# A two-layer trunk on one core: how the low parts of the weight tiles are made

## Chip, core and metric

The kernel runs on one core of a Trainium2 chip. The metric is the device time of one execution in microseconds. A time is the median of a few runs; a profile is one execution taken by the hardware profiler.

## What is computed

The reference is a trunk of two layers over 1024 tokens of width 1024, all in float32. The first layer mixes by a gated linear recurrence and by stick-breaking attention in parallel, the second by a gated convolution of 31 taps. After each mixer stands an MLP with squared ReLU, which holds most of the multiplications:

```python
def sq_relu_mlp(h, w1, w2):
    a = jax.nn.relu(h @ w1)
    return (a * a) @ w2

# D_MODEL = 1024, SEQ = 1024, D_FF = 4096, DEPTH = 2
for layer in range(DEPTH):
    if layer % 2 == 0:
        x = x + lru_sb_mixer(rms_norm(x, ev_norm_g[j]), ev_w_in[j], ..., ev_w_out[j])
    else:
        x = x + conformer_conv_module(rms_norm(x, od_norm_g[j]), od_pw1_w[j], ..., od_pw2_b[j])
    x = x + sq_relu_mlp(rms_norm(x, mlp_norm_g[layer]), mlp_w1[layer], mlp_w2[layer])
return rms_norm(x, final_g)
```

## The kernel before

The tokens are worked in two chunks, a and b, of 512. A float32 product is made of three passes of TensorE in the type float32r: every operand is split into a high part (its value in float32r) and a low part (what is left), and low x high, high x low and high x high are added in PSUM (`mm3`, lines 154 to 156).

A weight unit is 128 x 1024 elements. Two units are loaded at once by SP into a raw tile of 128 x 2048 (`raw`, two buffers). For each unit ScalarE casts the raw tile into the high part `wh` (line 101 for rows, 122 for columns), and VectorE subtracts the high part from the raw tile into the low part `wl` (lines 102 and 123). `wh` and `wl` have four buffers each. `col_units` loads column tiles (w1 of the MLP; pw, the first pointwise product of the convolution module; xg and qk, the first layer's input projection). For w1 the two column tiles lie next to each other in DRAM, so a partition of the raw tile holds, for each of 8 k tiles, 256 columns, of which a unit takes 128; for the others the two units are apart in the raw tile. `row_units` loads four row tiles of 512 columns (w2 of the MLP, wo, and q, the second pointwise product). The four units of v, at the start, are rows too.

The MLP (`mlp`) is run once for each layer and chunk: a0, b0, a1, b1, in the trace by chunk as w1a, w2a, w1b, w2b. A step m1 makes one of 32 hidden tiles from one unit of w1: 24 matmuls, then on ScalarE a relu, a square into float32r and a square in float32 (lines 249 to 252), then VectorE's low part of the activation (line 253). A step m2 adds four hidden tiles' product with half of the rows of w2, from two units: 48 matmuls and four adds into the residual on VectorE (line 237). After the first hidden tiles the steps run in groups: m2, m2, m1, m1, m1, m1.

The 30 later taps of each convolution tile (line 644) are put into a list, `waiting`, and `paced` issues some behind each of certain VectorE instructions: the number given to it is the credit of one such instruction.

The program is written in one order, and a scheduler puts the instructions of each engine into the order in which that engine runs them; an engine runs its own list strictly in order. A tile's buffer is given to the next tile of its kind when its last reader is done. GpSimd (POOL) has short work: the root of the norms (lines 184 to 186) and, in attention, a column of ones ahead of each scan (line 507) or a carried value (line 509).

Of the kernel before, what the change touches and what calls it, by code (L numbers as in the profile page):

```python
# [8 lines left out]
F32 = mybir.dt.float32  # L9
F32R = mybir.dt.float32r  # L10
BF16 = mybir.dt.bfloat16
AF = mybir.ActivationFunctionType
ALU = mybir.AluOpType
PSUM = bass.MemoryType.PSUM

P = 128
D = 1024
S = 1024
C = 512          # tokens in a chunk
NCH = S // C  # L20
KT = D // P      # k tiles of the model width
NH = 2           # halves of the model width
TT = C // P      # token tiles in a chunk
FF = 4096
KCONV = 31
HALO = KCONV - 1
G = 4            # hidden tiles in a group of the MLP
RMS_EPS = 1e-6
# [3 lines left out]
def tile_hybrid_trunk(  # L32
# [37 lines left out]

# [1 line left out]
    ident = cp.tile([P, P], F32, name="ident")  # L72
# [10 lines left out]

# [1 line left out]
    waiting, credit = [], [0.0]  # L85
# [7 lines left out]

# [1 line left out]
    def raw_tile(name):  # L95
        return wp.tile([P, 2048], F32, tag="raw", bufs=2, name=name)

    def split_w(raw, name):
        hi = wp.tile([P, 1024], F32R, tag="wh", bufs=4, name=f"wh_{name}")
        lo = wp.tile([P, 1024], F32R, tag="wl", bufs=4, name=f"wl_{name}")  # L100
        A.copy(hi, raw)  # L101
        paced(V.tensor_tensor(lo, raw, hi.bitcast(F32), op=ALU.subtract), 1)  # L102
        return hi, lo

    def col_units(w, c0, c1, name):
        """units of [k, 128 cols] for the col tiles from c0 and c1"""
        raw = raw_tile(f"raw_{name}")
        wk = w.rearrange("(k p) m -> p k m", p=P)
        if c1 == c0 + P:
            r3 = raw.rearrange("p (k m) -> p k m", k=KT)  # L110
            nc.sync.dma_start(r3, wk[:, :, c0:c0 + 2 * P])
            srcs = [r3[:, :, i * P:(i + 1) * P] for i in range(2)]
        else:
            r4 = raw.rearrange("p (i k m) -> p i k m", i=2, k=KT)
            srcs = [r4[:, i] for i in range(2)]
            for r, c in zip(srcs, (c0, c1)):
                nc.sync.dma_start(r, wk[:, :, c:c + P])

        def unit(i):
            hi = wp.tile([P, KT, P], F32R, tag="wh", bufs=4, name=f"wh_{name}{i}")  # L120
            lo = wp.tile([P, KT, P], F32R, tag="wl", bufs=4, name=f"wl_{name}{i}")
            A.copy(hi, srcs[i])  # L122
            paced(V.tensor_tensor(lo, srcs[i], hi.bitcast(F32), op=ALU.subtract), 2)  # L123
            return hi, lo
        return unit

    def row_load(w, k0, c0, name):
        """four k tiles, from row tile k0 or the ones listed"""
        raw = raw_tile(f"raw_{name}")
        ks = [k0 + i for i in range(4)] if isinstance(k0, int) else list(k0)  # L130
        i = 0
        while i < 4:
            n = 1
            while i + n < 4 and ks[i + n] == ks[i] + n:
                n += 1
            nc.sync.dma_start(raw[:, i * C:(i + n) * C].rearrange("p (k m) -> p k m", k=n),
                              w[ks[i] * P:(ks[i] + n) * P, c0:c0 + C].rearrange("(k p) m -> p k m", p=P))
            i += n
        return raw
# [5 lines left out]
    def row_units(w, k0, c0, name):  # L145
        """units of [2 k, 512 cols] for four k tiles from row tile k0"""
        raw = row_load(w, k0, c0, name)
        return row_unit(raw, 0, name) + row_unit(raw, 1, name)

    def mm3(acc, prs):  # L150
        """acc = sum over (lhsT hi/lo, rhs hi/lo) pairs, three passes each"""
        n = len(prs)
        for i, ((lh, ll), (rh, rl)) in enumerate(prs):
            T.matmul(acc, ll, rh, start=(i == 0), stop=False)  # L154
            T.matmul(acc, lh, rl, start=False, stop=False)  # L155
            T.matmul(acc, lh, rh, start=False, stop=(i == n - 1))  # L156
# [10 lines left out]

# [1 line left out]
    def rstd_of(xt, junk, name, vector=False):  # L169
        """xt: the two half tiles of 128 tokens; junk: scratch"""  # L170
        rs = sp.tile([P, 1], F32, tag="rs", name=f"rs_{name}")
# [17 lines left out]
    def norm(xt, g, g0, temp, name):  # L189
        """xt[token tile][half] -> the normed chunk, feature-major, split: [k] -> (hi, lo)"""  # L190
        res = []
        for _ in norm_parts(xt, g, g0, temp, name, TT, res):
            pass
        return res

    def norm_parts(xt, g, g0, temp, name, nt, res):
        """nt token tiles at a time, in steps of a feature tile"""
        rs = []
# [31 lines left out]

# [1 line left out]
    def rows_into_x(acts, ws, h, xt, name):  # L232
        for t in range(TT):
            acc = mm_ps(f"o_{name}{t}")
            mm3(acc, [((a[0][:, t * P:(t + 1) * P], a[1][:, t * P:(t + 1) * P]), w)
                      for a, w in zip(acts, ws)])
            paced(V.tensor_tensor(xt[t][h], acc, xt[t][h], op=ALU.add), 1.5)  # L237

# [1 line left out]
    def mlp(layer, hT, xt, name):  # L240
        acts, units = {}, {}

        def m1(f):
# [8 lines left out]
            A.activation(r, r, AF.Square)  # L252
            paced(V.tensor_tensor(lo, r, hi.bitcast(F32), op=ALU.subtract), 2.5)
            acts[f] = (hi, lo)
# [13 lines left out]

    NG = FF // (G * P)

    # ================= layer 0: recurrence and attention =================
    w_in = ev_w_in[0]
    y = [[None] * KT for _ in range(NCH)]      # [chunk][k tile], feature-major, split
    dp = ctx.enter_context(tc.tile_pool(name="dp", bufs=1, space=bass.MemoryType.DRAM))
    with tc.tile_pool(name="p1", bufs=1) as p1, tc.tile_pool(name="ps1", bufs=1, space=PSUM) as ps1:
# [16 lines left out]
        def load_vecs(groups, dma, name):  # L292
            """rows of 128 channels into columns"""
            rows = [(nm, ap.rearrange("a (k p) -> (a k) p", p=P)) for nm, ap in groups]
# [59 lines left out]

        # 4 * log_sigmoid(lam): min(lam, 0) - log1p(exp(-|lam|)), the log by its atanh series
        lam = vecs["lam"][0][:, vecs["lam"][1]:vecs["lam"][1] + 4]
# [23 lines left out]

        last = [None] * 4     # the previous chunk's last state

# [3 lines left out]
        def keep(c, k, t):  # L386
            """a k tile of the mixer's output: to DRAM, but for the last ones"""
            y[c][k] = t
# [4 lines left out]
        def lru(m, xr, gt):  # L393
# [3 lines left out]
            def decay(c):  # L397
# [8 lines left out]
                A.activation(nt[c], pr, AF.Sigmoid, bias=vec("ga_b", m))  # L406
                # t = tanh(log_a / 2): a = (1 + t) / (1 - t), 1 - a^2 = -4 t / (1 - t)^2
                A.activation(nt[c], nt[c], AF.Tanh, scale=c4[:, m:m + 1])
# [33 lines left out]
            with tc.high_priority(offset=140):  # L442
                decay(0)
                gate(0)
                ins = decay(1)
            # the square roots of both chunks together, for one load of their table
            with tc.issue_after(ins.ins):
# [29 lines left out]
        def attention(c, hp, q1, q2, ks):  # L477
            av = ps1.tile([P, C], F32, tag="av", bufs=1, name=f"av{hp}{c}")
            order = None
            for tt in range(TT):  # L480
# [3 lines left out]
                while hi_s > 0:  # L484
# [5 lines left out]
                    for j in range(2):  # L490
# [4 lines left out]
                        with tc.high_priority(offset=1000):  # L495
                            T.matmul(z[:, :w], q1[j][:, ts_], k_[:, :w], start=True, stop=False)
                            T.matmul(z[:, :w], q2[hs, ts_], k_[hs, :w], start=False, stop=not diag)  # L497
                            if diag:
                                T.matmul(z[:, w - P:w], ident_b, mask, start=False, stop=True)
                        # the product of keep over the later keys, then times beta: the weights  # L500
                        ke = at(f"ke{nm}")
# [19 lines left out]
                        wts.append(ke)  # L521
                    # one token tile's sums at a time in the bank
                    with tc.issue_after(order) if order is not None else nullcontext():
# [12 lines left out]
        def qk_cols(hp):  # L536
            """split for products of two passes: q1 holds the high part twice, q2 the low part,
            ks the high and the low part"""
            u = col_units(w_in, 1024 + hp * P, 1536 + hp * P, f"qk{hp}")
# [28 lines left out]

# [1 line left out]
        def out_proj(cs, i, h):  # L570
# [35 lines left out]

    # ================= layer 1 pieces =================
    halo = cp.tile([P, KT, HALO], F32, name="halo")
# [26 lines left out]
    def conv(c, ms, u, cv):  # L635
        """put the taps of some channel tiles, in turn, among the waiting"""
        for m in ms:
# [10 lines left out]
    def layer_norm(c, cv, s):  # L648
        """steps; s gets the split result"""
        xh = []  # L650
# [60 lines left out]

    # ================= schedule of the two chunks =================
    def steps(todo, n=None, between=()):
        """run the list's steps up to the group n's second hidden tile, with others in between"""
        between = list(between)
# [74 lines left out]
```

## Time and profile before

| | |
|---|---|
| median of 3 runs | 2253.16 us (2252.9 to 2256.04) |
| profiled execution, span | 2252.2 us |
| TensorE, matmuls | 2219.5 us, 99% |
| VectorE | 1414.6 us, 63% |
| ScalarE | 953.6 us, 42% |
| GpSimd | 98.3 us, 4% |
| all DMA | 199.24 MB |

The page gives the profiled execution's span and no other time of it; the median of the runs is 1.0 us above the span. Busy times are sums over an engine's instructions. A matmul's end is modelled, and successive matmuls overlap: one of 512 columns is shown with 0.39 us and the next starts 0.23 us later. So the distance of two starts is what a matmul costs. In the timeline a row has its start, its duration, the engine, the line, the operation and the tiles, and in brackets the idle time before it with what ended it.

### The profile page before, as it was taken

What the parts mean: (1) busy time and instruction counts of PE and PEld (TensorE: products, weight loads), DVE (VectorE), ACT (ScalarE), POOL (GpSimd) and SP (SyncE); (2) the same over time, 40 slices, a digit from 0 to 9 for tenths busy, and PEclk for the clock granted to TensorE, in tenths of its full rate; (3) what the DMA queues carried; (4) which work ended last, traced back from release to release, by engine and by line L of the source; (5) the groups of instructions that cost most, each with busy time, mean ns of one, the idle gap of its engine ahead of it and who ended that gap; (6) DMA issues with size and microseconds to landing.
All of it is one profiled execution on the core that took longest, in us unless ns stands there. A gap on an engine that the chain in (4) does not pass through costs nothing.

```text
span 2252.2 us, 25937 instructions
## 1 busy us (share of the span) xinstructions
PE 2219.5 (99%) x10180; PEld 1768.3 (79%) x10180; DVE 1414.6 (63%) x1934; ACT 953.6 (42%) x1506; POOL 98.3 (4%) x280
## 2 busy tenths in 40 slices
PE   7999999999999999999999999999999999999998
PEld 5866766678888888888888888788888888888886
DVE  4376777866443444579889765899886555444344
ACT  4456566555333333433333363433333545333332
POOL 1000000001000000200000010300000001000000
PEclk9999999999999999999999999999999999999999
DMA  4211002312222232432222223322222224222222
GB/s 157 56 41 36 34 29 85 117 38 75 94 94 93 94 104 92 114 94 94 94 94 94 94 94 94 84 94 94 94 94 94 94 94 146 97 94 94 94 94 75
DMA packets 172009, 199.24 MB, mean 88 GB/s; under 512 B 5648, under 2 KB 120688, under 8 KB 171888
## 3 DMA queue, kind: packets, MB, share of 16 engines
q1 hardware_dynamic: 171872, 197.59, 27.4%
q8 instruction: 80, 1.31, 0.2%
q14 instruction: 41, 0.34, 0.0%
q10 hardware_dynamic: 16, 0.00, 0.0%
HBM read 190.23 MB, written 7.34 MB: 88 GB/s over the span
## 4 chain that ended last, share of the span: by engine, by line
PE 95%; DVE 2%; ACT 1%; issue 1%; DMA 0%; POOL 0%; SPq 0%; DVEq 0%; POOLq 0%; ACTq 0%
PE o_a L154 5%; PE o_a L156 5%; PE o_b L155 5%; PE o_b L154 5%; PE o_b L156 5%; PE o_a L155 5%; PE m_a L154 5%; PE m_b L155 5%; PE m_a L156 5%; PE m_a L155 5%; PE m_b L156 5%; PE m_b L154 5%; PE av L527 2%; PE z L497 1%; PE o_wo L154 1%; PE wt L519 1%
## 5 line engine op out<-in xcount | busy, mean ns | idle before, releaser
L644 DVE SCALAR_TENSOR_TENSOR cv<-u,dwT,cv 128x512 f32<-128x512 f32 x480 | 340.6, 757 | 0.2
L154 PE MATMUL o_a<-wh_w2a,al_a 128*128 128x512 f32 x512 | 202.8, 396 | 0.0
L155 PE MATMUL o_a<-wl_w2a,ah_a 128*128 128x512 f32 x512 | 202.7, 396 | 0.0
L156 PE MATMUL o_b<-wh_w2b,ah_b 128*128 128x512 f32 x512 | 202.6, 396 | 0.0
L154 PE MATMUL o_b<-wh_w2b,al_b 128*128 128x512 f32 x512 | 202.6, 396 | 0.0
L155 PE MATMUL o_b<-wl_w2b,ah_b 128*128 128x512 f32 x512 | 202.5, 396 | 0.0
L156 PE MATMUL o_a<-wh_w2a,ah_a 128*128 128x512 f32 x512 | 202.1, 396 | 0.0
L122 ACT CAST wh_w1b<-raw_w1b 128x1024 fp32r<-128x1024 f32 x64 | 67.3, 1052 | 220.5 <-PE o_b L156 210.6
L122 ACT CAST wh_w1a<-raw_w1a 128x1024 fp32r<-128x1024 f32 x64 | 67.3, 1053 | 214.1 <-PE o_a L156 204.0
L102 DVE TENSOR_TENSOR wl_w2a<-raw_w2a,wh_w2a 128x1024 fp32r<-128x1024 f32 x64 | 78.3, 1224 | 122.9 <-ACT wh_w2a L101 122.8
L102 DVE TENSOR_TENSOR wl_w2b<-raw_w2b,wh_w2b 128x1024 fp32r<-128x1024 f32 x64 | 81.1, 1268 | 117.2 <-ACT wh_w2b L101 117.1
L237 DVE TENSOR_TENSOR xr<-o_a,xr 128x512 f32<-128x512 f32 x128 | 87.7, 688 | 81.5 <-PE o_a L156 81.4
L237 DVE TENSOR_TENSOR xr<-o_b,xr 128x512 f32<-128x512 f32 x128 | 88.0, 688 | 77.2 <-PE o_b L156 77.1
L156 PEld LDWEIGHTS o_b<-wh_w2b,ah_b 128*128 128x128 f32 x512 | 96.2, 188 | 23.1
L156 PEld LDWEIGHTS o_a<-wh_w2a,ah_a 128*128 128x128 f32 x512 | 96.3, 188 | 23.0
L155 PEld LDWEIGHTS o_b<-wl_w2b,ah_b 128*128 128x128 f32 x512 | 96.2, 188 | 22.9
L154 PEld LDWEIGHTS o_a<-wh_w2a,al_a 128*128 128x128 f32 x512 | 96.2, 188 | 22.9
L154 PEld LDWEIGHTS o_b<-wh_w2b,al_b 128*128 128x128 f32 x512 | 96.2, 188 | 22.8
L155 PEld LDWEIGHTS o_a<-wl_w2a,ah_a 128*128 128x128 f32 x512 | 96.3, 188 | 22.7
L249 ACT ACTIVATE r_b<-m_b 128x512 f32<-128x512 f32 x64 | 38.3, 599 | 167.2 <-PE m_b L156 167.2
L249 ACT ACTIVATE r_a<-m_a 128x512 f32<-128x512 f32 x64 | 38.3, 599 | 162.8 <-PE m_a L156 162.8
L123 DVE TENSOR_TENSOR wl_w1b<-raw_w1b,wh_w1b 128x1024 fp32r<-128x1024 f32 x64 | 78.0, 1221 | 38.2 <-ACT wh_w1b L122 38.2
(535 smaller groups left out, 5327.4 us busy)
## 6 DMA issues: line engine op xcount, KB each, us to landing
raw_w1a<-in_mlp_w_dram SPq DMA_DIRECT2D x32, 1024.0 KB, 5.3
raw_w2a<-in_mlp_w_dram SPq DMA_DIRECT2D x32, 1024.0 KB, 5.0
raw_w1b<-in_mlp_w_dram SPq DMA_DIRECT2D x32, 1024.0 KB, 5.4
raw_w2b<-in_mlp_w_dram SPq DMA_DIRECT2D x32, 1024.0 KB, 5.0
raw_pw<-in_od_pw_w_dram SPq DMA_DIRECT2D x32, 512.0 KB, 5.4
raw_q<-in_od_pw_w_dram SPq DMA_DIRECT2D x8, 1024.0 KB, 5.0
raw_wo<-in_ev_w_out_dram SPq DMA_DIRECT2D x6, 768.0 KB, 5.4
xa<-in_x_dram SPq DMA_DIRECT2D x16, 256.0 KB, 5.4
```

What stands on the lines that cost most here:

```text
L102: paced(V.tensor_tensor(lo, raw, hi.bitcast(F32), op=ALU.subtract), 1)
L122: A.copy(hi, srcs[i])
L123: paced(V.tensor_tensor(lo, srcs[i], hi.bitcast(F32), op=ALU.subtract), 2)
L154: T.matmul(acc, ll, rh, start=(i == 0), stop=False)
L155: T.matmul(acc, lh, rl, start=False, stop=False)
L156: T.matmul(acc, lh, rh, start=False, stop=(i == n - 1))
L237: paced(V.tensor_tensor(xt[t][h], acc, xt[t][h], op=ALU.add), 1.5)
L249: A.activation(r, acc, AF.Relu)
L497: T.matmul(z[:, :w], q2[hs, ts_], k_[hs, :w], start=False, stop=not diag)
L519: T.transpose(pt[:, b * P:(b + 1) * P], ke[:, b * P:(b + 1) * P], ident)
L527: ins = T.matmul(av[j * 64:j * 64 + 64, tt * P:(tt + 1) * P], vt[lo_s // P + b][:, hc:hc + 64], wts[j][:, b * P:(b + 1) * P], start=(diag ...
L644: waiting.append(lambda k=k, m=m: V.scalar_tensor_tensor(cv[m], u[m][:, k:k + C], dwT[:, k * KT + m:k * KT + m + 1], cv[m], op0=ALU.mult, ...
```

## The change

For all weight units but those of v, VectorE's subtraction goes. A new function, `rest`, takes its place: ScalarE copies the high part with scale -1 into the low part's tile, and a DMA issued by GpSimd adds the raw tile to it. 332 units are made so. As the subtractions no longer stand on VectorE, they no longer give credit to the taps, and the credits of the residual's add and of the activation's low part are raised. Nothing else of the computation is changed.

```diff
+    def rest(lo, raw, hi):
+
+        A.activation(lo, hi.bitcast(F32), AF.Copy, scale=-1.0)
+        Q.dma_start(lo, raw, accum_op=ALU.add)
+
     def split_w(raw, name):
...
         A.copy(hi, raw)
-        paced(V.tensor_tensor(lo, raw, hi.bitcast(F32), op=ALU.subtract), 1)
+        if name[0] == "v":
+            V.tensor_tensor(lo, raw, hi.bitcast(F32), op=ALU.subtract)
+        else:
+            rest(lo, raw, hi)
         return hi, lo
...
             A.copy(hi, srcs[i])
-            paced(V.tensor_tensor(lo, srcs[i], hi.bitcast(F32), op=ALU.subtract), 2)
+            rest(lo, srcs[i], hi)
             return hi, lo
...
-            paced(V.tensor_tensor(xt[t][h], acc, xt[t][h], op=ALU.add), 1.5)
+            paced(V.tensor_tensor(xt[t][h], acc, xt[t][h], op=ALU.add), 2.5)
...
-            paced(V.tensor_tensor(lo, r, hi.bitcast(F32), op=ALU.subtract), 2.5)
+            paced(V.tensor_tensor(lo, r, hi.bitcast(F32), op=ALU.subtract), 6)
```

The scheduler's order moves with it. ScalarE in a group of the last MLP, from the second m1 step to the casts of the two units for the second m2 step (r_b, ah_b: relu and squares of a hidden tile; the numbers are the program's own and differ from one program to the other). Before:

```order
L249 ACTIVATE r_b_15969<-m_b_15940 128x512
L101 CAST wh_w2b_16056<-raw_w2b_16050 128x1024
L251 ACTIVATE ah_b_15971<-r_b_15969 128x512
L252 ACTIVATE r_b_15969<-r_b_15969 128x512
L249 ACTIVATE r_b_16005<-m_b_15976 128x512
L251 ACTIVATE ah_b_16007<-r_b_16005 128x512
L252 ACTIVATE r_b_16005<-r_b_16005 128x512
L101 CAST wh_w2b_16118<-raw_w2b_16116 128x1024
L249 ACTIVATE r_b_16043<-m_b_16014 128x512
L101 CAST wh_w2b_16122<-raw_w2b_16116 128x1024
```

ScalarE at the same place in the changed program (line 106 is the cast, line 100 the negation, 257 to 260 are the relu and the squares), first around the cast of the second unit of the first m2 step:

```order
L106 CAST wh_w2b_15213<-raw_w2b_15211 128x1024
L257 ACTIVATE r_b_15128<-m_b_15098 128x512
L106 CAST wh_w2b_15218<-raw_w2b_15211 128x1024
L100 ACTIVATE wl_w2b_15214<-wh_w2b_15213 128x1024
L259 ACTIVATE ah_b_15130<-r_b_15128 128x512
L100 ACTIVATE wl_w2b_15219<-wh_w2b_15218 128x1024
L260 ACTIVATE r_b_15128<-r_b_15128 128x512
```

and then around the two units of the second m2 step:

```order
L257 ACTIVATE r_b_15204<-m_b_15174 128x512
L259 ACTIVATE ah_b_15206<-r_b_15204 128x512
L106 CAST wh_w2b_15281<-raw_w2b_15279 128x1024
L106 CAST wh_w2b_15286<-raw_w2b_15279 128x1024
L260 ACTIVATE r_b_15204<-r_b_15204 128x512
L100 ACTIVATE wl_w2b_15282<-wh_w2b_15281 128x1024
L100 ACTIVATE wl_w2b_15287<-wh_w2b_15286 128x1024
```

The negation of a unit does not follow its cast at once: the other unit's cast stands between them, and for the first m2 step a relu too.

GpSimd in attention, in the third head pair (ke: the tile that gets its column of ones; xgt and lh: other short copies). Before:

```order
L507 MEMSET ke_2601 128x1
L507 MEMSET ke_2616 128x1
L507 MEMSET ke_2630 128x1
L507 MEMSET ke_2648 128x1
L507 MEMSET ke_2663 128x1
L470 COPY xgt_3093<-xgt_3065 128x3
L507 MEMSET ke_2684 128x1
L438 COPY lh_2416<-xc_2374 128x1
```

and in the changed program (line 101 is the DMA, 515 the column of ones):

```order
L515 MEMSET ke_2613 128x1
L101 DMA wl_qk_3309<-raw_qk_3232 128x1024
L515 MEMSET ke_2628 128x1
L515 MEMSET ke_2642 128x1
L515 MEMSET ke_2660 128x1
L515 MEMSET ke_2675 128x1
L478 COPY xgt_3106<-xgt_3078 128x3
L515 MEMSET ke_2696 128x1
L101 DMA wl_wo_3905<-raw_wo_3901 128x1024
L446 COPY lh_2426<-xc_2384 128x1
```

The issues of the accumulating DMAs stand among the columns of ones. ScalarE loads a function table 12 times in the changed program and 10 times before.

## Rows read from the trace of the kernel before

**Rows 1.** The page: busy time of the engines, and the chain's shares.
```profile
PE 2219.5 (99%) x10180; PEld 1768.3 (79%) x10180; DVE 1414.6 (63%) x1934; ACT 953.6 (42%) x1506; POOL 98.3 (4%) x280
...
PE 95%; DVE 2%; ACT 1%; issue 1%; DMA 0%; POOL 0%; SPq 0%; DVEq 0%; POOLq 0%; ACTq 0%
```

**Rows 2.** Waits of TensorE: in total, times, longest.
```profile
PE nps_e L211 <- DVE xn_e L206: 8.3, 2, 7.1
...
PE nps_ma L211 <- DVE hl_ma L217: 2.9, 2, 2.6
```

**Rows 3.** Stretches: length, busy time of each engine, clock, DMA share, GB/s.
```profile
120.00:520.00 400.00, 394.97 (x2069) 276.85 (x2070) 296.54 (x434) 236.07 (x466) 20.05 (x114) 1.00 0.17 56
1440.00:1460.00 20.00, 17.10 (x81) 13.52 (x80) 20.00 (x20) 8.24 (x11) 11.24 (x7) 1.00 0.29 79
1890.00:2235.00 345.00, 345.00 (x1502) 281.66 (x1501) 139.60 (x160) 121.94 (x164) 3.51 (x6) 1.00 0.29 95
```

**Rows 4.** Groups by line: VectorE's subtraction; count, busy, mean ns, idle before.
```profile
L102 DVE TENSOR_TENSOR wl_w2a<-raw_w2a,wh_w2a 128x1024 fp32r<-128x1024 f32 x64 | 78.3, 1224 | 122.9 <-ACT wh_w2a L101 122.8
```

**Rows 5.** Timeline of ScalarE in the last MLP.
```profile
1939.45 1.05 ACT L122 CAST wh_w1b<-raw_w1b 128x1024 fp32r<-128x1024 f32 x1 [8.74 <-PE o_b L156]
...
1946.85 1.05 ACT L101 CAST wh_w2b<-raw_w2b 128x1024 fp32r<-128x1024 f32 x1
...
1951.76 0.60 ACT L249 ACTIVATE r_b<-m_b 128x512 f32<-128x512 f32 x1 [2.67 <-PE m_b L156]
1952.25 1.04 ACT L101 CAST wh_w2b<-raw_w2b 128x1024 fp32r<-128x1024 f32 x1
1953.19 0.63 ACT L251 ACTIVATE ah_b<-r_b 128x512 fp32r<-128x512 f32 x1
...
1959.60 1.05 ACT L101 CAST wh_w2b<-raw_w2b 128x1024 fp32r<-128x1024 f32 x1 [0.48 <-DMA raw_w2b<-in_mlp_w_dram]
1962.64 0.60 ACT L249 ACTIVATE r_b<-m_b 128x512 f32<-128x512 f32 x1 [1.99 <-PE m_b L156]
...
1983.64 1.05 ACT L122 CAST wh_w1b<-raw_w1b 128x1024 fp32r<-128x1024 f32 x1 [8.74 <-PE o_b L156]
```

**Rows 6.** Timeline of SP, VectorE and TensorE in the same group.
```profile
1941.79 13.16 SPq L136 DMA_DIRECT2D raw_w2b<-in_mlp_w_dram  x2
...
1953.33 1.23 DVE L102 TENSOR_TENSOR wl_w2b<-raw_w2b,wh_w2b 128x1024 fp32r<-128x1024 f32 x1 [3.51 <-ACT wh_w2b L101]
...
1960.68 1.23 DVE L102 TENSOR_TENSOR wl_w2b<-raw_w2b,wh_w2b 128x1024 fp32r<-128x1024 f32 x1 [0.83 <-ACT wh_w2b L101]
...
1973.88 0.39 PE L155 MATMUL o_b<-wl_w2b,ah_b 128*128 128x512 f32 x1
...
1975.28 0.39 PE L155 MATMUL o_b<-wl_w2b,ah_b 128*128 128x512 f32 x1
```

**Rows 7.** The page: DMA queue; issues by tile with KB and us to landing.
```profile
q1 hardware_dynamic: 171872, 197.59, 27.4%
...
raw_w1a<-in_mlp_w_dram SPq DMA_DIRECT2D x32, 1024.0 KB, 5.3
raw_w2a<-in_mlp_w_dram SPq DMA_DIRECT2D x32, 1024.0 KB, 5.0
...
out_dram<-fo SPq DMA_DIRECT2D x16, 256.0 KB, 2.0
```

**Rows 8.** Groups by line on GpSimd: longest instruction, and a short one.
```profile
L694 POOL TENSOR_TENSOR xr<-xr,pw2b 128x512 f32<-128x512 f32 x16 | 25.8, 1646 | 23.1 <-DVE hl_ma L217 15.9 <-DMA pw2b<-in_od_pw_b_dram 7.3
...
L186 POOL TENSOR_TENSOR rs_f<-rs_f,mhalf 128x1 f32<-128x1 f32 x8 | 4.4, 550 | 0.7
```

**Rows 9.** Groups by line on ScalarE: loading a function table.
```profile
L503 ACT ACT_TABLE_LOAD x4 | 5.1, 1283 | 0.2 <-PE av L527 0.2
```

**Rows 10.** The chain in order of time, in attention: start, us, what.
```profile
382.00 0.95 ACT wh_wo L101
...
389.69 0.31 ACT ke L503
```

## Prediction

> **What bounds the kernel now.** I read the page's busy table first, then the waits of TensorE, then stretches, then one group of the MLP in time order. TensorE is busy 99% of the span, and the chain that ended last is 95% TensorE [rows 1]. Its own named waits are a few microseconds each; the longest is on the norm at the start, and after 520 us only the one on nps_ma is over 1 us [rows 2]. Over the last MLP, 1890 to 2235 us, it is busy 345.00 of 345.00 us while VectorE, from which the change takes work, is busy 139.60 [rows 3]. So shorter VectorE work has little to give. What can change the time is whether a low part still arrives before TensorE asks for it.
>
> **What is removed and added.** VectorE loses 332 subtractions (64 each for the four w1 and w2 groups, 32 for pw, 16 for q, 12 for wo, 8 each for xg and qk; the 4 of v stay) at about 1.22 us [rows 4], some 405 us of its 1414.6. ScalarE gains 332 negations of 128x1024. The nearest row is the cast of the same shape, 1.05 us [rows 5]: 349 us, which takes it from 953.6 to about 1300 of 2252 us. GpSimd's queue gains 332 accumulating DMAs of 512 KB, the only new kind of work. 332 times 512 KB is 174 MB against 197.59 MB now, which took 27.4% of the sixteen engines [rows 7]; counted as twice the bytes, since both operands are read, it is another 48%. The engines are not full. Latency is the question, not the total.
>
> **The path of a low part.** Before: cast, subtraction. After: cast, negation, GpSimd's issue, DMA. I call d the time from the end of a negation to the landing of its sum. No row shows it. From below: the rate in the queue's row is 197.59 MB in 27.4% of 16 x 2252.2 us, 20 GB/s an engine, 320 GB/s in all; a 256 KB store lands in 2.0 us [rows 7], of which 0.82 is data at that rate, so 1.18 us is fixed, and 512 KB would be 1.18 + 1.64 = 2.8 us. From above: two operands read are 1 MB, and a 1 MB load lands in 5.0 us [rows 7]; with GpSimd's longest instruction, 1.65 us, ahead of it that is 6.65 us [rows 8]. For w1 the raw piece of a partition is cut into 8 runs of 512 B (the raw tile holds two column tiles side by side). Eight of GpSimd's short instructions, 0.55 us each [rows 8], would be 4.4 us, and d there 9.4 us at most. I take 5.0 + 0.5 = 5.5 us for both kinds, nearest to the row that moves as many bytes, behind one short GpSimd instruction.
>
> The Trainium skill, DMA: Bandwidth & Descriptors, section Anatomy of one DMA — SWDGE (gpsimd) path, fits a GpSimd-issued DMA with about 2.0 us plus bytes over 436 GB/s. By that fit, as an estimate, d would be 3.2 us and the sum would be that of the first rival below; no run here shows such a DMA. Collectives: The Full Stack (the Trainium skill), section The bandwidth ceiling: the fold count and why AG ≠ RS ≠ AR, says that a DMA that adds runs at about half the rate of one that copies, because of two source reads. With that, an estimate, d is 4.4 us, still the rival.
>
> **How much d is hidden.** I follow one group of the last MLP. A group is four m1 steps and two m2 steps: its third m1 unit is cast at 1939.45 and the next group's at 1983.64, 44.2 us apart [rows 5]. Two m1 steps lie between the relus at 1951.76 and 1962.64 [rows 5], 5.44 us each, which leaves 11.2 us for an m2 step. A0, A1 and B0, B1 are the two units of its two m2 steps. Both raw tiles of w2 and the second w1 pair go in turn through one raw buffer: B's load starts only when A1's low part is there. Before, A1 is subtracted at 1953.33 for 1.23 us [rows 6], B's load follows, B0's cast is at 1959.60 [rows 5] and its subtraction ends at 1961.91 [rows 6]. TensorE first reads that low part at 1973.88 and B1's at 1975.28 [rows 6]: 12 us to spare.
>
> After, with ScalarE in its new order (ScalarE's fences in the section on the change): A1's cast still waits for the relu at 1951.76 and runs at 1952.25 [rows 5], ending 1953.29. Then stand A0's negation (1.05), a square (0.63 [rows 5]) and A1's negation (1.05), to 1956.02. So A0's negation, whose cast was done long before, is queued behind a cast that waits for TensorE. The DMA lands at 1956.02 + d. The load of B takes 5.06, from 1941.79 [rows 6] to the cast at 1946.85 [rows 5] in the load before it. Then two casts (2.10), a square (0.63) and B0's negation (1.05): 1964.86 + d, and landed 1964.86 + 2d; B1 at 1965.91 + 2d. Against 1973.88 and 1975.28 the slack is 9.0 - 2d and 9.4 - 2d. **The point from which it decides is d = 4.5 us**; each microsecond above costs two in a group. One more loop: A's load waits for the low part of the third m1 unit, cast at 1939.45 [rows 5], negated by 1941.55, landed 1941.55 + d. With load and cast A0 is ready at 1947.66 + d, and this pushes A1 from d = 4.6 on, one for one.
>
> At d = 5.5 a group stalls TensorE by 2 x 5.5 - 9.0 + 5.5 - 4.6 = 2.9 us. The four MLPs have 8 groups each, 32: **+92 us**. At the lower bound it is 0; at the upper ones 2 x 6.65 - 9.0 + 9.4 - 4.6 = 9.1 us a group, +291. Each stall moves the rest of the program, because TensorE has no idle to take it up. Elsewhere I cost it at nothing: in pw each unit is wanted three units of 5.44 us after its buffer is free, and in q and wo the steps of 11.2 us have no load waiting for a sum just ahead of them; both cover 2.1 + 5.5 us. If that cover is gone (d above 9), they stall too.
>
> **Attention.** ScalarE is busy 236.07 of the 400 us from 120 to 520 [rows 3]; 28 negations (xg, qk, wo) and, by the new order, two more table loads (12 instead of 10) of 1.28 us [rows 9] come to 32 us there. At most all of it lies on the path, at least nothing. The chain is ScalarE's alone from a wh_wo cast at 382.00 to 389.69 [rows 10]; three negations and the two loads there make 3 x 1.05 + 2 x 1.28 = 5.7, so I take **+6 us**. GpSimd's column of ones for a scan now stands behind DMA issues (its fences); those issues wait for a negation, and VectorE's scan for the column. That is in the 0 to 32.
>
> **What is won.** From 1440 to 1460 us VectorE is busy 20.00 of 20.00 and TensorE only 17.10 [rows 3]: subtractions of pw stand between the taps. They leave, and I take **-3 us**; the most would be that and TensorE's other VectorE waits after 60 us, some 8 in all. The pacing gives 44 taps a group instead of 34 (6 x 4 + 2.5 x 8 against 4.5 x 4 + 8 x 2); 44 taps of 0.7 us with the adds still fit into 44 us, so no gain or loss is put down.
>
> **Sum:** 2252.2 + 92 + 6 - 3 = 2347.2 us of span; the median of the runs, 2253.16, is 1.0 above the span, so **2348 us**.
>
> **Rival 1, the sums land in time (not slower).** d is below 4.5. For it: the store's row gives 2.8 us. Against it: stores read one operand only, and no GpSimd issue is in them. Then the MLPs lose nothing, attention gives 0 to 15, pw up to -8: 2245 to 2268 us, about 2256 in the middle. It ends faster only if attention is hidden too; then the 20 us at 1440 decide, at about 2248.
>
> **Rival 2, GpSimd or the pieces are the bound.** d for w1 is near 9.4 and for rows near 6.65. For it: eight times the pieces in 128 DMAs. Against: loads of w1 with 1 KB runs land as fast as those of w2 with longer ones, 5.3 and 5.0 us [rows 7]. Price: +291 + 6 - 3, 2547 us; more if GpSimd needs over 11 us for each of the four w1 units of a group, since it then fills the 44 us itself.
>
> **Rival 3, the change does not unload VectorE** as it says, because taps and adds set its order anyway. TensorE does not wait for it, so this gives the time of rival 1.
>
> **How the numbers follow.** About 0.2%, 4.5 us, is what a measurement of this kernel can tell from no change. The forecast (d 4.5 to 6.5, 2268 to 2490 us) has a chance of 0.43; rival 1 with rival 3, 0.34; rival 2, 0.23, half of it above 2550. Of the 0.34, 0.09 is faster than 2248.7, 0.17 within 0.2%, 0.08 slower. So faster 0.09, same 0.17, slower 0.74. The range leaves out half of rival 2 and most of the faster cases: 2250 to 2550.
>
> **What would show it.** Right: TensorE gets waits on wl_w2 low parts, each of 2 to 4 us and once a group, at the second m2 step of it; B's raw load is issued some 9 us after A1's cast begins instead of 2.3; VectorE falls to about 1010 us and ScalarE rises to about 1300. Wrong: no wait of TensorE on a low part (then d is under 4.5 and rival 1 holds); waits before m1 steps or GpSimd busy for most of the MLP (rival 2); a loss that sits before 520 us (then the attention term is the one that is mis-sized).

## The result, and the profile after

The changed kernel takes **2600.28 us** (median of 4 runs, 2597.99 to 2602.44); the kernel before, beside it, 2253.03 us. The ratio is 1.154, 95% interval 1.152 to 1.155: 347 us slower. The forecast was 2348 us in a range up to 2550, so the direction held and the size did not.

The page of the kernel after: busy time of the engines, the DMA queues, and the shares of the chain that ended last (compare [rows 1] and [rows 7]).

```profile
PE 2345.5 (90%) x10180; PEld 1822.2 (70%) x10180; DVE 1025.7 (40%) x1602; ACT 1268.0 (49%) x1840; POOL 466.5 (18%) x612
...
q0 software_dynamic: 162496, 174.08, 46.5%
q1 hardware_dynamic: 171872, 197.59, 23.5%
...
DMA 44%; PE 35%; issue 12%; POOL 4%; ACT 4%; DVE 1%; POOLq 0%; SPq 0%; DVEq 0%; ACTq 0%
```

VectorE fell to 1025.7 and ScalarE rose to 1268.0 us, close to the 1010 and 1300 foretold: the change does unload VectorE. But the chain, 95% TensorE before, is now 44% DMA. The new queue q0 has the share that was estimated, 46.5% against 48%. Over the span as a whole no engine and no queue is full, and still 344 us were added.

Waits of TensorE in the kernel after: in total, times, longest (compare [rows 2]).

```profile
PE o_a L163 <- DMA wl_w2a<-raw_w2a: 60.0, 35, 3.5
PE o_b L163 <- DMA wl_w2b<-raw_w2b: 57.9, 39, 4.3
PE m_b L162 <- DMA wl_w1b<-raw_w1b: 41.4, 14, 6.4
PE m_a L162 <- DMA wl_w1a<-raw_w1a: 29.0, 12, 5.1
```

The waits on low parts of w2 are there, of up to 4.3 us, as foretold (and in the group followed below B's load leaves 9.75 us after A1's cast begins, where some 9 were foretold); beside them stand waits of up to 6.4 us on low parts of w1, which the forecast did not have. They add up to 188 us. Another 126 us are TensorE's busy time itself, 2345.5 for 2219.5 [rows 1], on the same 10180 matmuls; the granted clock in the next view goes with it.

Stretches of the kernel after: length, busy time of PE, PEld, DVE, ACT and POOL, granted clock, DMA share, GB/s (compare [rows 3]; 2250 to 2307 is one group of the last MLP, 2258 to 2276 the part of it with three sums of w1).

```profile
120.00:520.00 400.00, 391.42 (x2022) 273.68 (x2021) 269.75 (x406) 254.51 (x485) 33.73 (x127) 0.98 0.29 76
...
2250.00:2307.00 57.00, 48.35 (x189) 37.79 (x189) 8.11 (x12) 22.67 (x28) 9.67 (x8) 0.91 0.78 149
...
2258.00:2276.00 18.00, 14.21 (x52) 11.19 (x51) 1.38 (x2) 7.64 (x9) 4.64 (x3) 0.81 1.01 148
```

In this group the granted clock is no longer 1.00 but 0.91, a mean of pieces at 2.4 and at 1.2 GHz: behind a wait of 3.79 us that ends at 2267.54, matmuls start 0.43 us apart until 2272.8 us, and 0.23 us apart after that. So some of the waits cost more than their own length on TensorE. Whether that also lengthens the span depends on who sets the group, and that is the next question.

**Who sets the group.** SP's own waits, in total, times, longest: two rows of the kernel before, then the same loads after.

```profile
SPq L136 <- DVE wl_w1a L123: 190.9, 18, 12.3
...
SPq L136 <- DVE wl_w2b L102: 124.6, 16, 11.9
```

```profile
SPq L144 <- DMA wl_w2b<-raw_w2b: 268.8, 16, 19.0
...
SPq L144 <- DMA wl_w1a<-raw_w1a: 252.2, 18, 19.3
```

Loads always waited for a raw buffer. What frees it was VectorE's subtraction and is now the landing of an accumulating DMA. The chain in order of time shows what follows (kernel after, one group of the last MLP; start us, us, what; TensorE's pieces left out).

```profile
2250.39 7.32 DMA raw_w1b<-in_mlp_w_dram
...
2262.26 9.53 DMA wl_w1b<-raw_w1b
2271.92 7.15 DMA raw_w2b<-in_mlp_w_dram
...
2284.29 5.87 DMA wl_w2b<-raw_w2b
...
2300.12 6.74 DMA wl_w2b<-raw_w2b
2307.00 7.39 DMA raw_w1b<-in_mlp_w_dram
```

SP's issues of the two row loads in the same group (start us, us, operation; A leaves at 2271.92, B at 2290.28), to be read against the 13.16 us of [rows 6].

```profile
2271.92 18.73 SPq L144 DMA_DIRECT2D raw_w2b<-in_mlp_w_dram  x2
```

It is a closed loop. One of the two raw buffers takes, in turn, one pair of w1 tiles, row half A and row half B, while the other buffer holds the other pair, whose last unit is split only after both row halves. From one w1 load to the next are 2307.00 - 2250.39 = 56.61 us, and they consist of three times the same: a load (7.40, 7.17, 5.12 us until the cast starts), ScalarE's two casts and two negations with GpSimd's pick-up (4.47, 5.20, 4.72), and the second sum until the next load leaves (9.66, 5.99, 6.88). Loads 19.7, ScalarE 14.4, sums 22.5: together 56.6. TensorE needs 44.2 for the group, so it is not the bound there any more. (From 2290.29 to 2300.10 the page's chain runs through TensorE's matmuls. I read the sum that leaves at 2300.12 as released by its negation, which ends at 2299.83: the other two sums, too, leave 0.29 and 0.30 us behind theirs.) A slower clock or a longer TensorE step should then not show in the span as long as it fits into the loop; that was not tried by itself.

### The profile page after: what moved, and what is told of

Its sections match the earlier page's. It is cut to its first block, busy times and chain, and to the rows that moved or that the text cites. A ratio compares the mean times of both kernels' runs of the same rounds, so it can differ in the third digit from the quotient of the medians.

```text
span 2596.3 us, 27011 instructions
## 1 busy us (share of the span) xinstructions
PE 2345.5 (90%) x10180; PEld 1822.2 (70%) x10180; DVE 1025.7 (40%) x1602; ACT 1268.0 (49%) x1840; POOL 466.5 (18%) x612
## 3 DMA queue, kind: packets, MB, share of 16 engines
q0 software_dynamic: 162496, 174.08, 46.5%
## 4 chain that ended last, share of the span: by engine, by line
DMA 44%; PE 35%; issue 12%; POOL 4%; ACT 4%; DVE 1%; POOLq 0%; SPq 0%; DVEq 0%; ACTq 0%
DMA wl_w2b<-raw_w2b 6%; DMA raw_w2a<-in_mlp_w_dram 6%; DMA raw_w2b<-in_mlp_w_dram 6%; DMA wl_w2a<-raw_w2a 6%; DMA wl_w1b<-raw_w1b 5%; DMA wl_w1a<-raw_w1a 5%; DMA raw_w1b<-in_mlp_w_dram 4%; DMA raw_w1a<-in_mlp_w_dram 3%; PE av L535 2%; PE wt L527 1%; PE z L505 1%; PE xg L162 1%; PE xg L163 1%; PE xg L164 1%; PE o_wo L162 1%
## 5 line engine op out<-in xcount | busy, mean ns | idle before, releaser
L163 PE MATMUL o_a<-wl_w2a,ah_a 128*128 128x512 f32 x512 | 215.8, 422 | 60.0 <-DMA wl_w2a<-raw_w2a 60.0
L106 ACT CAST wh_w2b<-raw_w2b 128x1024 fp32r<-128x1024 f32 x64 | 65.7, 1044 | 277.9 <-DMA raw_w2b<-in_mlp_w_dram 277.9
L261 DVE TENSOR_TENSOR al_b<-r_b,ah_b 128x512 fp32r<-128x512 f32 x64 | 45.6, 713 | 365.4 <-ACT r_b L260 365.4
L106 ACT CAST wh_w2a<-raw_w2a 128x1024 fp32r<-128x1024 f32 x64 | 65.6, 1045 | 254.0 <-DMA raw_w2a<-in_mlp_w_dram 251.4
L261 DVE TENSOR_TENSOR al_a<-r_a,ah_a 128x512 fp32r<-128x512 f32 x64 | 44.2, 690 | 346.6 <-ACT r_a L260 346.5
L163 PEld LDWEIGHTS o_a<-wl_w2a,ah_a 128*128 128x128 f32 x512 | 102.0, 199 | 97.8 <-DMA wl_w2a<-raw_w2a 56.6
L101 POOL DMA_DIRECT2D wl_w1a<-raw_w1a x64 | 99.8, 1562 | 255.3 <-ACT wl_w1a L100 224.8
L101 POOL DMA_DIRECT2D wl_w1b<-raw_w1b x64 | 100.0, 1563 | 232.4 <-ACT wl_w1b L100 230.9
L101 POOL DMA_DIRECT2D wl_w2a<-raw_w2a x64 | 55.7, 876 | 452.5 <-ACT wl_w2a L100 325.2
L101 POOL DMA_DIRECT2D wl_w2b<-raw_w2b x64 | 55.4, 869 | 446.0 <-ACT wl_w2b L100 420.7
L162 PE MATMUL m_b<-hh_mb,wl_w1b 128*128 128x512 f32 x256 | 107.4, 420 | 28.8 <-DMA wl_w1b<-raw_w1b 26.2
```

What stands on the lines that cost most here:

```text
L101: Q.dma_start(lo, raw, accum_op=ALU.add)
```

## The experiments

The theory to be tested: the loop through one raw buffer sets the group. Its rivals: the moved pacing, ScalarE's order, the rate at which GpSimd and the DMA engines put sums through, and the landing of a sum as such, buffers or not. All ratios are to the kernel before, run beside the experiment.

**Parts of the change without any DMA.** The first keeps only the pacing numbers:

```diff
-        if name[0] == "v":
-            V.tensor_tensor(lo, raw, hi.bitcast(F32), op=ALU.subtract)
-        else:
-            rest(lo, raw, hi)
+        V.tensor_tensor(lo, raw, hi.bitcast(F32), op=ALU.subtract)
...
-            rest(lo, srcs[i], hi)
+            V.tensor_tensor(lo, srcs[i], hi.bitcast(F32), op=ALU.subtract)
```

> VectorE's subtraction is back for every unit; only the numbers that pace the background work (2.5 behind a row step, 6 behind a hidden tile, nothing behind a subtraction) stay as the change set them. Loop theory (the group is set by one raw buffer through which the row halves A and B and one column pair pass in turn, each held until its accumulating DMA has landed): with no such DMA the loop falls to about 30 us and TensorE sets the group again, so 2253 us, give or take 10. Rival, the moved background work: the loss stays, 2500 us or more.

2251.91 us, ratio 0.999 (0.998 to 0.9999). The pacing costs nothing, and that rival falls; it even gains some 2 us, which the forecast had put at nothing, and this is the lowest median of all versions run.

The second keeps ScalarE's negations as well:

```diff
-        Q.dma_start(lo, raw, accum_op=ALU.add)
+        V.tensor_tensor(lo, raw, lo.bitcast(F32), op=ALU.add)
```

> ScalarE's negation stays, VectorE adds the raw tile to it, no DMA. This is the extra ScalarE work of the change (328 negations of 1.05 us and their place between the casts) by itself, with the same waits of VectorE behind it. Loop theory: a unit holds its buffer some 1.3 us for the sum in place of 5 to 9.5, the loop is about 3 x (5.1 + 5.5) = 32 us, under TensorE's 44.2, so 2253 to 2290 us. Rival, ScalarE's order (casts queued behind negations): most of the 347 us stays, over 2450.

2252.81 us, ratio 0.9995 (0.9985 to 1.0004). So the 332 negations (the 328 above is a slip) of 1.05 us cost nothing in the whole. Their order is not tried here: the scheduler gives this kernel another one, with each row unit's negation ahead of the other's cast in the last MLP. The copy below keeps the order of the changed kernel.

**One kind of unit alone.** The DMA for the names that begin with w1 only, then for w2 only:

```diff
-        if name[0] == "v":
+        if not name.startswith('w1'):
             V.tensor_tensor(lo, raw, hi.bitcast(F32), op=ALU.subtract)
...
-            rest(lo, srcs[i], hi)
+            if name.startswith('w1'):
+                rest(lo, srcs[i], hi)
+            else:
+                V.tensor_tensor(lo, srcs[i], hi.bitcast(F32), op=ALU.subtract)
```

> Only the low parts of the w1 units (128 of the 332) go by negation and accumulating DMA, all others by VectorE's subtraction. Loop theory: A and B hold the buffer some 9 us each (load 5.1, two casts and subtractions 3.8), the column pair 21.5 as in the changed kernel, together 39.5, under the 44.2 us of TensorE's group: 2253 to 2310 us, the rest being waits for single low parts. Rival, a price for each DMA or each byte (GpSimd, the DMA engines, the clock): about half of the 347 us or, by landing times, 60%: 2420 to 2460.

> Only the low parts of the w2 units (128 of the 332) go by negation and accumulating DMA, all others by VectorE's subtraction. Loop theory: A and B hold the buffer 16 to 17 us each (load 5.1, ScalarE 5.2, sum 5 to 6), the column pair some 10, together 42 to 44, at TensorE's 44.2: 2253 to 2320 us. The two halves of the change would then cost far less by themselves than together. Rival, a price for each DMA or byte: 40 to 50% of the 347 us, 2390 to 2430.

w1 alone 2285.31 us, ratio 1.014 (1.012 to 1.015); w2 alone 2280.41 us, ratio 1.012 (1.010 to 1.013): 31 and 26 us. Together they are 57 us, where the changed kernel loses 347. A price for each DMA or byte would add up. A loop that is no longer than TensorE's group with either half, and longer with both, gives just this. The last MLP shows it: six groups lie between these two w1 loads, first with w1 alone, then with w2 alone.

```profile
1946.04 14.99 SPq L119 DMA_DIRECT2D raw_w1b<-in_mlp_w_dram  x2
...
2214.41 0.37 SPq L119 DMA_DIRECT2D raw_w1b<-in_mlp_w_dram  x1
```

```profile
1956.03 1.02 SPq L119 DMA_DIRECT2D raw_w1b<-in_mlp_w_dram  x2
...
2224.82 0.37 SPq L119 DMA_DIRECT2D raw_w1b<-in_mlp_w_dram  x1
```

That is 44.7 and 44.8 us a group, near TensorE's 44.2; the same six groups of the changed kernel (2193.76 to 2535.61) take 57.0.

**Pieces of 512 B.** The w1 pair in two contiguous tiles, so that a unit's source is 4 KB of a partition in one piece (the pair is then loaded by two DMAs of 512 KB):

```diff
-        if c1 == c0 + P:
+        if c1 == c0 + P and not name.startswith("w1"):
```

> The changed kernel, but the pair of w1 column tiles is loaded by two DMAs, each tile to a contiguous 4 KB of a partition (as the xg and qk pairs are, whose sums land after 4.8 and 4.5 us). The accumulating DMA then reads 4 KB in a piece and not 8 pieces of 512 B. Loop theory: the column pair's sum falls from 9.4 to about 5.5 us, the loop from 56.6 to about 53, 32 groups: about 2480 us. Rival, the bytes that are added set the landing and not the pieces: no change, 2600.

2382.00 us, ratio 1.057 (1.054 to 1.059): 218 us of the 347 are back, 100 more than expected. Issues of this kernel (operation, count, KB each, median us to landing), after the same rows of the changed kernel:

```profile
wl_w1a<-raw_w1a POOLq DMA_DIRECT2D x64, 512.0 KB, 9.1
raw_w2a<-in_mlp_w_dram SPq DMA_DIRECT2D x32, 1024.0 KB, 5.4
wl_w2a<-raw_w2a POOLq DMA_DIRECT2D x64, 512.0 KB, 4.7
raw_w1b<-in_mlp_w_dram SPq DMA_DIRECT2D x32, 1024.0 KB, 7.0
...
raw_w2b<-in_mlp_w_dram SPq DMA_DIRECT2D x32, 1024.0 KB, 6.9
wl_w2b<-raw_w2b POOLq DMA_DIRECT2D x64, 512.0 KB, 5.1
```

```profile
wl_w1a<-raw_w1a POOLq DMA_DIRECT2D x64, 512.0 KB, 5.7
...
raw_w2b<-in_mlp_w_dram SPq DMA_DIRECT2D x32, 1024.0 KB, 5.0
wl_w2b<-raw_w2b POOLq DMA_DIRECT2D x64, 512.0 KB, 4.6
```

Its own SP rows give the loop:

```profile
2035.16 4.83 SPq L125 DMA_DIRECT2D raw_w1b<-in_mlp_w_dram  x4
2050.35 16.50 SPq L144 DMA_DIRECT2D raw_w2b<-in_mlp_w_dram  x2
2082.59 1.63 SPq L125 DMA_DIRECT2D raw_w1b<-in_mlp_w_dram  x2
```

47.4 us instead of 56.6. The three sums take 5.9 us less of the loop than in the changed kernel, 4.1 of it in the one of w1, and the loads 3.5 less. Of these, 2.3 are w1's, whose first cast now waits only for the first of the two smaller DMAs: that part belongs to the edit. A's load takes 1.0 less (over all groups the median of raw_w2b went from 6.9 to 5.0; in the changed kernel those of raw_w2a and raw_w1b were 5.4 and 7.0, where [rows 7] has 5.0 and 5.3 for their like); with sums that are over sooner, fewer of them run beside a load, which may be the cause, but that was not tried by itself. My expectation had only w1's sum.

**A third raw buffer**, in the last MLP alone (its pool gives up four tiles of another kind for it):

```diff
+        if third and name.startswith("raw_w2") and name.endswith("0"):
+            return third[0].tile([P, 2048], F32, tag="raw3", bufs=1, name=name)
         return wp.tile([P, 2048], F32, tag="raw", bufs=2, name=name)
...
```

> The changed kernel with a third raw buffer in the last of the four MLPs alone: row half A has a buffer of its own there. Loop theory: B and the column pair make a loop of 17 + 21.5 = 38.5 us, under TensorE's 44.2, so the last MLP's groups fall from 56.6 to 44 to 48 us (the rest waits for single low parts) and the time by 8 x 9 to 12 us: 2505 to 2530 us. Rival, the rate at which sums go through (GpSimd or the DMA engines): the groups stay at 56, 2590 to 2600.

2527.87 us, ratio 1.121 (1.119 to 1.123): 72 us less than the changed kernel, from one MLP of four. SP's rows there:

```profile
2195.16 9.35 SPq L123 DMA_DIRECT2D raw_w1b<-in_mlp_w_dram  x2
...
2238.69 11.33 SPq L123 DMA_DIRECT2D raw_w1b<-in_mlp_w_dram  x2
...
2284.31 10.12 SPq L123 DMA_DIRECT2D raw_w1b<-in_mlp_w_dram  x2
...
2327.56 11.17 SPq L123 DMA_DIRECT2D raw_w1b<-in_mlp_w_dram  x2
```

The groups take 43.5, 45.6 and 43.3 us, about TensorE's 44.2, with the same sums in the same pieces through the same queue. The rate at which GpSimd and the DMA engines put sums through is not the bound, and neither are the four buffers of the low parts, which are as before.

**The loop opened everywhere.** The sum takes the tile from DRAM a second time, so the raw buffer is free after the cast:

```diff
-        Q.dma_start(lo, raw, accum_op=ALU.add)
+        Q.dma_start(lo, raw if src is None else src, accum_op=ALU.add)
...
```

> The accumulating DMA takes the tile from DRAM a second time and not from the raw buffer, which so comes free with its cast, in all four MLPs; the same number of DMAs and bytes added. Loop theory: the loop through the raw buffer is about 3 x 8 = 25 us, TensorE sets the group but for waits for low parts that land late: 2260 to 2400 us. Rival, the rate at which sums go through, or their landing as such: 2550 or more, and longer with more reads from DRAM.

2283.82 us, ratio 1.013 (1.011 to 1.014): 316 of the 347 us are back. The sums land in 6.1 to 7.6 us in the MLPs; yet between its first loads at 1994.16, 2038.34, 2082.53 and 2126.72 us the last MLP runs in groups of 44.2. In that MLP the DMA share is 0.95. The same source, with the MLPs' units alone and the others back on VectorE:

```diff
-        if name[0] == "v":
+        if name[:2] not in ("w1", "w2"):
             V.tensor_tensor(lo, raw, hi.bitcast(F32), op=ALU.subtract)
...
-            rest(lo, srcs[i], hi, wk[:, :, (c0, c1)[i]:(c0, c1)[i] + P])
+            if name[:2] != "w1":
+                V.tensor_tensor(lo, srcs[i], hi.bitcast(F32), op=ALU.subtract)
+            else:
+                rest(lo, srcs[i], hi, wk[:, :, (c0, c1)[i]:(c0, c1)[i] + P])
```

> Only the MLPs' 256 units go by negation and accumulating DMA, and the DMA takes its tile from DRAM, so that no raw buffer waits for it; the other 76 are back on VectorE's subtraction. Loop theory: the MLP groups run at TensorE's 44.2 us as in before, and the 29 us that the same source cost in the whole kernel lay ahead of the first MLP: 2250 to 2260 us, with half the subtractions' work gone from VectorE and nothing won by it. Rival, waits for low parts in the MLPs: 2270 to 2285.

2259.14 us, ratio 1.002 (1.001 to 1.003): 4 us slower than before, where 0 was the middle of what was expected. With the loop open the MLPs hide 256 accumulating DMAs almost wholly, and gain nothing from VectorE's rest, as [rows 3] had said.

**A copy in place of the sum.** The same transfers through the same buffers, without the adding. The low part is then the raw tile itself, so this kernel leaves out the subtraction and does not compute the product; only its time is of use.

```diff
-        Q.dma_start(lo, raw, accum_op=ALU.add)
+        Q.dma_start(lo.bitcast(F32), raw)
```

> The same DMAs from GpSimd, from the same buffers into the same tiles behind the same negation, but as plain copies, without adding (the low part is then the raw tile). Loop theory with the adding as its price: copies land in about half the time (2.3 to 3 us for a row unit, about 4.5 for a column unit), the loop falls from 56.6 to about 45, 2260 to 2320 us. Rival, GpSimd's issuing and the waits around a DMA as such: landing times and the 2600 us stay.

2263.70 us, ratio 1.004 (1.002 to 1.005). Its issues:

```profile
wl_w1a<-raw_w1a POOLq DMA_DIRECT2D x64, 512.0 KB, 4.7
...
wl_w2a<-raw_w2a POOLq DMA_DIRECT2D x64, 512.0 KB, 2.9
```

It is the adding that makes the landing long, and the landing that closes the loop. Sums as fast as these copies would have given the time of the prediction's first rival. This is also the cleanest of the experiments: by the two traces all 1840 instructions of ScalarE, 1602 of VectorE, 612 of GpSimd and 10180 matmuls stand in the same order as in the changed kernel. So ScalarE's order, the two more table loads and the number of GpSimd's issues cost at most the 9 us that are left; the other rival falls with it, and the loss hangs on how long the DMAs take. (The kernels with a third buffer and with the source in DRAM were given other orders on ScalarE.)

**The units outside the MLPs.** All 76 of them, and (with the condition `name[:2] == "pw"` instead) the 32 of pw alone:

```diff
-        if name[0] == "v":
+        if not (name[:2] not in ("w1", "w2") and name[0] != "v"):
...
```

> The MLPs' 256 units are back on VectorE's subtraction; the other 76 of the change (recurrence and attention, the output projection, pw and the second convolution product) go by negation and accumulating DMA. Loop theory: the start of the first MLP comes some 20 us later, as in the changed kernel's trace (518.1 for 498.5 us), less a few us in the pw stages: 2262 to 2278 us, so that over 320 of the 347 us belong to the MLPs. Rival, a price for each unit: 76 of 332 units, 80 us, 2330.

> Only the 32 units of the convolution's input products (pw) go by negation and accumulating DMA, all others by VectorE's subtraction; the pacing numbers are those of the change. This is the stage where VectorE, and not TensorE, was read as the bound between 1440 and 1460 us. If taking 32 subtractions of 1.22 us off VectorE pays there, 2246 to 2251 us (the pacing alone gave 2252). Rival, the low part's 5.8 us of landing is waited for in the same stage: 2253 to 2265.

The 76 units: 2268.74 us, ratio 1.007 (1.005 to 1.008), 14 us; so, if the two parts add up, 333 of the 347 us lie in the MLPs. The changed kernel's trace says the same: from its first w1 load to its last, each MLP takes 75.7, 78.6, 89.3 and 88.7 us longer than in the kernel before, 332 together. The 32 of pw: 2254.89 us, ratio 1.0002 (0.9993 to 1.001): nothing won, against the first expectation. The stretch that was read as VectorE's, in this kernel (columns as in [rows 3]):

```profile
1440.00:1460.00 20.00, 17.22 (x75) 13.72 (x75) 10.18 (x14) 8.18 (x11) 12.54 (x11) 0.91 0.47 80
```

VectorE is busy 10.18 us there instead of 20.00, and TensorE does no more than before (17.22 for 17.10). In the kernel before, TensorE did wait there for VectorE, for 2.9 us in two waits; the longer one is for the low part of a norm (hl_ma), which VectorE made at 1452.91, behind a subtraction of pw and a tap:

```profile
1450.02 2.30 DVE L123 TENSOR_TENSOR wl_pw<-raw_pw,wh_pw 128x1024 fp32r<-128x1024 f32 x1
...
1453.70 0.55 PE L211 MATMUL nps_ma<-ident,xn_ma 128*128 128x128 f32 x3 [2.63 <-DVE hl_ma L217]
```

With pw's DMA that wait is gone, and another stands in its place:

```profile
1440.13 10.08 POOL L705 TENSOR_TENSOR xr<-xr,pw2b 128x512 f32<-128x512 f32 x8 [8.74 <-DMA pw2b<-in_od_pw_b_dram]
1450.17 1.64 POOL L101 DMA_DIRECT2D wl_pw<-raw_pw  x2
...
1454.82 0.47 PE L165 MATMUL pv<-hh_ob,wl_pw 128*128 128x512 f32 x1 [2.78 <-DVE hl_ma L228]
```

The row names hl_ma, but VectorE ends that one at 1454.83, when the matmul has begun. What it needs is a low part of pw. Its negation ended at 1436.49, but in GpSimd's list eight additions of a bias (pw2b) stand ahead of its DMA; so the sum is issued at 1450.17 and lands at 1454.69, a d of 18.2 us. In the changed kernel's rows the same wait, 2.8 us long, has the name of wl_pw. So the rival of the expectation holds, in its time (2253 to 2265) and in its wait: what VectorE gave back, a late sum took. (Against the pacing alone, 0.999, this is no gain either; the two intervals overlap.)

## Why the prediction failed, by its own steps

The step that failed is the stall of a group in the MLPs: 2.9 us forecast (+92 for 32 groups), 12.4 measured (332 in all). The mechanism was the one foretold; the terms in it, d above all, were too small.

- **Direction, and what bounds the kernel: right.** Shorter VectorE work had nothing to give, and the landing of the low parts decided. The point d = 4.5 us was passed.
- **d, the time from the end of a negation to the landing: mis-sized.** In the group above, the second negations end at 2261.97, 2283.99 and 2299.83 us (ScalarE's rows, below), and the next loads leave at 2271.92, 2290.28 and 2307.00. So d is 9.95 us for w1, 6.29 and 7.17 for rows, where 5.5 was taken for all three. That of w1 and the second of the rows passed even the upper bounds, 9.4 and 6.65, by about half a microsecond. By the page's medians (4.7 and 5.1 us from issue to landing) a row sum has a d of 5.0 to 5.4, an estimate, near what was taken; but the buffer is free only with the second sum of a pair, which runs beside the first and lands later.

```profile
2260.91 1.06 ACT L100 ACTIVATE wl_w1b<-wh_w1b 128x1024 fp32r<-128x1024 f32 x1
...
2282.95 1.04 ACT L100 ACTIVATE wl_w2b<-wh_w2b 128x1024 fp32r<-128x1024 f32 x1
...
2297.83 2.00 ACT L100 ACTIVATE wl_w2b<-wh_w2b 128x1024 fp32r<-128x1024 f32 x2
```

- **The worst choice was one value for both kinds.** The text had the 8 runs of 512 B and a bound of 9.4 for them, and then took the value of the row kind, "nearest to the row that moves as many bytes". The run with contiguous w1 tiles shows the runs of 512 B at 9.1 us against 5.7.
- **The raw loads were kept at 5.06 us** [rows 5, 6]. With sums in flight on the same engines w1's and A's took 7.32 and 7.15 us; B's, until its cast, took 5.12. The forecast had checked that the engines were not full, which is true of the span (q1 and q0 together 70%), and concluded that only latency counts. In stretches they are full: the DMA share is 1.01 from 2258 to 2276 us, and from 2296 to 2299 it is 0.00. So the latency of one transfer grew with the others beside it.
- **The formula itself was good.** With the measured sizes, 6.29 + 7.17 - 9.0 for the two row sums, 9.95 - 4.6 for w1, and 7.15 - 5.06 for A's load give 11.9 us a group; the loop gives 56.6 - 44.2 = 12.4. With its own sizes it gave 2.9. Of the 9 us between, 4.4 are w1's landing, 2.5 the rows', 2.1 the load.
- **One leg of the loop was left out.** The text followed A to B and the third w1 unit to A, each against the time at which TensorE asks. It did not follow B to the next w1 load, by which the loop closes and lateness is carried into the next group. In steady groups this matters little for the size, as the two results show (that they come within 0.5 us of each other is in part luck, as the slacks of the formula were read from the kernel before); it matters for the reading: with a closed loop the price is the loop's length less TensorE's, and nothing inside TensorE's group can take it up.
- 32 groups of 12.4 us would be 397 us; measured are 332 for the MLPs. In each there are only seven steps from one group's w1 loads to the next one's, and not all of them are steady (the first of the first MLP is 3.8 us longer than before). At the other end, the 2490 us that the text gives for d = 6.5 do not follow from its formula, which gives 5.9 us a group there, some 2445 us.
- **Won in pw: -3 forecast, 0 measured**, as shown above. That TensorE waited for VectorE there was right. The step that failed is the cover in pw, where the landing was costed at nothing ("both cover 2.1 + 5.5 us"): one d was 18.2 us there, because eight GpSimd instructions stood ahead of the issue where the text allowed for one, and TensorE waited for that sum as long as it had waited for VectorE.
- **Rival 1** failed on its condition (d below 4.5); the copy, whose row transfers land in 2.9 us, meets it and has its time. **Rival 2** had the right signs (waits ahead of m1 steps, the pieces) and the nearest price, 2547 us; its "GpSimd as the bound" was wrong, since the third buffer took the loss away with GpSimd's work unchanged. **Rival 3** is refuted by VectorE's busy time.

**Attention: +6 forecast, about +13 measured.** TensorE's first product of the first MLP starts at 545.85 us instead of 533.01:

```profile
533.01 0.47 PE L154 MATMUL m_a<-hh_m,wl_w1a 128*128 128x512 f32 x1 [0.87 <-ACT hh_m L216]
```

```profile
545.85 0.47 PE L162 MATMUL m_a<-hh_m,wl_w1a 128*128 128x512 f32 x1
```

With the 76 units outside the MLPs alone it starts at 545.26, with the copies at 541.35, with the negations alone, summed by VectorE, at 534.63. So 4.5 us hang on the adding. The other 8 come with the copies too, by the new order or by the landing of a DMA as such; the negations with the two more table loads, in another order, cost under 2. The forecast had put ScalarE's work there and no landing. (The first load of that MLP leaves 19.6 us later, but it waits for a raw buffer, and TensorE does not wait as long.) The column tiles' loads wait for the sums in this stage too: those of xg leave at 77.13 and 106.91 us instead of 71.90 and 99.38. How the 13 us divide further, the granted clock (0.98 there against 1.00 in [rows 3]) included, was not separated.

## What to carry to other kernels

When the consumer that frees a buffer is moved to a slower path, write down every tile that passes through that buffer in one period, and add up load, work and release over the whole circle: the price is that sum less the period, and each half of a change can be free while both together are not. Price a transfer of a kind that the trace lacks by its pieces as well as its bytes, keep two kinds apart, look at what stands ahead of its issue in the engine's list, and let loads grow when new traffic runs beside them. An engine that is full in a stretch costs no more there than others are seen to wait for it, and work moved off it can be waited for just as long elsewhere.

## What the runs showed of the hardware

Adding cost about twice copying. In the two kernels whose sums and copies have the same number of packets, the queue's rows are, with sums (contiguous w1 tiles) and then with copies (w1 in runs of 512 B):

```profile
q0 software_dynamic: 47808, 174.08, 40.0%
```

```profile
q0 software_dynamic: 47808, 174.08, 22.3%
```

Of 2379.9 and 2261.3 us these are 952 and 504 us of the sixteen engines, a ratio of 1.9. The Trainium skill, Collectives: The Full Stack, section The bandwidth ceiling: the fold count and why AG ≠ RS ≠ AR, has the adding step of a ring of cores at about half the rate of the copying one, because an add needs two source reads; these two rows of one core agree. By the fit of the Trainium skill, DMA: Bandwidth & Descriptors, section Anatomy of one DMA — SWDGE (gpsimd) path, 512 KB take 3.2 us, an estimate. The row copies landed in 2.9 us and the row sums in 4.6 to 5.1, so of these that fit holds for the copies only.

A sum out of runs of 512 B was cut into far more packets than a copy out of the same runs: 162,496 in the changed kernel, 47,808 with the plain copy. It also held GpSimd longer at its issue (operation of GpSimd in the changed kernel; count, busy us, mean ns):

```profile
L101 POOL DMA_DIRECT2D wl_w1b<-raw_w1b x64 | 100.0, 1563 | 232.4 <-ACT wl_w1b L100 230.9 <-ACT r_b L257 0.8 <-issue 0.5
...
L101 POOL DMA_DIRECT2D wl_w2b<-raw_w2b x64 | 55.4, 869 | 446.0 <-ACT wl_w2b L100 420.7 <-PE o_b L164 13.1 <-PE m_b L162 11.4
```

The bound of 4.4 us for GpSimd's share of such a DMA, made from eight of its short instructions [rows 8], was much too high: the issue takes 1.56. Most of the 9.1 us lies behind it.
